# A 100-byte tile taken out of the constants of a one-core transformer block

## The chip, the cores and the metric

The kernel runs on one core of a Trainium2 chip. The metric is device microseconds of that core, from the first to the last work of one execution, and lower is better. Five kinds of worker appear in the profile: TensorE (PE for the matmuls, PEld for the loading of their weights), VectorE (DVE), ScalarE (ACT), GpSimd (POOL), and SyncE (SP), which issues nearly all transfers.

## The reference

One decoder layer on a sequence of 1024 tokens with 1024 features, in float32. What is computed, with the norms and reshapes left out:

```python
xn = rmsnorm(h, norm_mix_g)
proj = xn @ w_in                                  # 1024 x 2568: q, k, v, u, vg, forget gates
att = forgetting_attention(q, k, v, log_sigmoid(proj[..., G_END:] + b_forget))   # 8 heads of 64, causal
sg = chunked_spatial_gating(u, vg, v_gain, w_s, b_s)    # gelu(u) * (tril(w_s) @ rmsnorm(gelu(vg)) + b_s)
h = h + concatenate([att, sg]) @ w_out
a, g = split(causal_depthwise_conv3(rmsnorm(h) @ w_up) + conv_b)     # w_up: 1024 x 5632
h = h + (silu(g) * a) @ w_down                    # w_down: 2816 x 1024
out = rmsnorm(h)
```

## The kernel before

The kernel keeps float32 accuracy on TensorE by splitting every operand into a high part, rounded to the type float32r, and a low part, which is the operand less its high part. `split_w` does this for weights: a copy on ACT at line 392 and a subtraction on DVE at line 398. Each product then takes three matmuls: high by high, high by low, low by high. The large products are also cut into 2 x 2 blocks with seven block products in place of eight (Strassen's scheme, with the operands named A11 to S4 on the side of the weights and B11 to T4 on the side of the activations). So the matmuls come in runs of twelve (four blocks of 128 rows by three parts), nearly all with 128 rows, 128 columns of stationary weights and 512 columns of moving data.

The stages, in order of time:

- Projections (lines 495 and 637), to about 200 us. In `tmul`, line 495, the stationary operand is a block of x and the moving one is a block of weights. In `product`, line 637, it is the other way round. The split weights go through a ring of six buffers, `RTAG = ("wy", "wy", "whl", "whl", "whl", "whl")`.
- Attention (lines 1009 to 1058), gating, and the output projection, whose matmuls are worked in between as filling (line 1125, tile `fl`), to about 470 us.
- Up projection, 22 steps of seven products (`up_b` and `up_a`, line 1457, with convolution and SiLU on ACT and DVE). Weights A11 and A12 are in `wha`, the five others in `whb`; activations are in `xB11`, `xB21`, `xT2`, `xT3`, `xT1`, `xT4`, `xB22`. The order in a step is S2, S3, the A11 of the next step, S1, A22, the A12 of the next step, S4.
- Down projection (`dprod`, line 1652): seven products of 11 x 12 matmuls each, with `wha` stationary and `whb` moving.

The order of instructions up to the output projection is made by a planner (class `Pace`, method `settle`). It lists all instructions of this part, gives each a modelled duration, and simulates the engines; the order that it finds is then fixed for each engine. The later part runs in the order in which it is written.

On-chip memory is handed out by pools. The pools `cst` (constants), `sml`, `early`, `upl`, `xtp`, `pst` and `dn` lie on the left and grow upward; `raws`, `late` and `upr` lie on the right and grow downward from the top. In the allocation list of the program, addresses are bytes within each of the 128 partitions:

- Below 1152 lie a scratch area of 1024 bytes and four small constants.
- The constants take 2144 bytes, each tile rounded up to a multiple of 32: `cp` 768, `eps`, `one` and `lim` 32 each, `ident` 512, `maskb` 256, `pad` 128 (100 bytes rounded up), `ng1`, `rstd1` and `ss1` 32 each, `gms` 256, `ss2` 32.
- The small pool takes twelve tiles of 32 bytes. So `early`, and later `upl`, begin at 1152 + 2144 + 384 = 3680, which is 7 x 512 + 96.
- On the right, `raws` begins at 212960 = 415 x 512 + 480.

The tiles of `early`, `upl`, `late`, `raws` and `upr` that matmuls read all have sizes that are multiples of 512 bytes, and a slice of 128 float32 columns is 512 bytes. So every such operand on the left begins at the remainder 96 modulo 512, and every one on the right at 480 (the forget gates' weights at line 720, in steps of 256 bytes, are the exception). Which tile is where:

| left (96) | right (480) |
|---|---|
| `wy`, `gg`, `V`, `H`, `x1`, `x2`, `t2`, `t3`, `t01` | `whl`, `pt`, `A`, `G`, `raw` |
| `xB11`, `xB21`, `xT2`, `xT3`, `wha`, `sg` | `xT1`, `xT4`, `xB22`, `whb` |

`ident`, the identity matrix for transposes, lies among the constants at 2016, ahead of `pad`, with remainder 480. `pad` at line 370 is written once, by a memset on DVE at line 371, and read by nothing.

Of the kernel before, what the change touches and what calls it, by code (L numbers as in the profile page):

```python
# [8 lines left out]
F32 = mybir.dt.float32  # L9
# [5 lines left out]
P = 128  # L15
# [275 lines left out]
def block_kernel(ctx: ExitStack, tc: tile.TileContext, xT, xtok, wuv, wv, wqk, wf, cpk, bfv,  # L291
                 ggain, g2r, gfr, wsp, woa, wos, wup, wdn, out):
    nc = tc.nc
    act, dve, pool, pe, sp = nc.scalar, nc.vector, nc.gpsimd, nc.tensor, nc.sync
    pace = Pace(tc)

    cst = pace.pool(ctx.enter_context(tc.tile_pool(name="cst", bufs=1)))
# [69 lines left out]
    pool.affine_select(out=maskb, in_=maskb, pattern=[[-1, P]], compare_op=ALU.is_ge,  # L367
                       fill=BIG, base=0, channel_multiplier=1)

    pad = cst.tile([P, 25], F32, name="pad")  # L370
    dve.memset(pad, 0.0)
    ng1 = cst.tile([P, 8], F32, name="ng1")
    dve.tensor_scalar(out=ng1, in0=g1, scalar1=-1.0, scalar2=None, op0=ALU.mult)
    rstd1 = cst.tile([P, 8], F32, name="rstd1")
# [1420 lines left out]
```

## Time and profile before

| | |
|---|---|
| median of the runs | 1088.05 us (1086.39 to 1088.16, 3 runs) |
| profiled execution, its own time | 1090.22 us |
| profiled execution, span | 1088.5 us |
| granted TensorE clock, mean | 0.993 |

The span goes from the first to the last instruction of the profiled execution; its own time also holds what lies around it. In rows of the profile that name tiles, the tile written stands left of the arrow and those read right of it; a matmul's row names the moving operand first and the stationary one second (`b<-wy,V`: `wy` moves, `V` is stationary), and only one name where both come from tiles of the same name.

### The profile page before, as it was taken

What the parts mean: (1) busy time and instruction counts of PE and PEld (TensorE: products, weight loads), DVE (VectorE), ACT (ScalarE), POOL (GpSimd) and SP (SyncE); (2) the same over time, 40 slices, a digit from 0 to 9 for tenths busy, and PEclk for the clock granted to TensorE, in tenths of its full rate; (3) what the DMA queues carried; (4) which work ended last, traced back from release to release, by engine and by line L of the source; (5) the groups of instructions that cost most, each with busy time, mean ns of one, the idle gap of its engine ahead of it and who ended that gap; (6) DMA issues with size and microseconds to landing.
All of it is one profiled execution on the core that took longest, in us unless ns stands there. A gap on an engine that the chain in (4) does not pass through costs nothing.

```text
span 1088.5 us, 14285 instructions
## 1 busy us (share of the span) xinstructions
PE 1067.7 (98%) x4885; PEld 867.8 (80%) x4885; DVE 906.9 (83%) x1391; ACT 574.4 (53%) x1006; POOL 239.5 (22%) x211
## 2 busy tenths in 40 slices
PE   9999999999999999998999999999999999999997
PEld 6888778788888877876888888888888888888885
DVE  6986599898888868998888998988989766897774
ACT  6657444477777746653444445344444544453653
POOL 0002124233362250063233233333332000000000
PEclk9999999999999999998999999999999999999999
DMA  9242236886674354222313323331322998333432
GB/s 338 87 141 96 89 112 170 257 265 184 191 226 146 120 200 164 76 80 98 136 59 117 115 94 100 107 118 67 119 104 76 304 329 276 107 97 93 141 117 94
DMA packets 64712, 158.16 MB, mean 145 GB/s; under 512 B 7672, under 2 KB 7936, under 8 KB 64640
## 3 DMA queue, kind: packets, MB, share of 16 engines
q1 hardware_dynamic: 64352, 156.70, 43.7%
q8 instruction: 38, 0.62, 0.2%
q10 hardware_dynamic: 288, 0.56, 0.1%
q14 instruction: 34, 0.28, 0.1%
HBM read 114.95 MB, written 42.27 MB: 144 GB/s over the span
## 4 chain that ended last, share of the span: by engine, by line
PE 83%; issue 7%; DVE 4%; DMA 3%; POOL 2%; ACT 1%; SPq 0%; POOLq 0%; DVEq 0%; ACTq 0%
PE s L1457 20%; PE b L1457 14%; PE s L1652 11%; PE b L1652 8%; PE s L495 6%; PE b L495 5%; PE fl L1125 4%; PE po L1049 3%; PE tr L1030 3%; PE b L637 2%; PE s L637 2%; PE lg L1010 2%; PE lg L1009 2%; DMA qd<-G 1%; PE s L720 1%
## 5 line engine op out<-in xcount | busy, mean ns | idle before, releaser
L1457 PE MATMUL s<-xT,whb 128*128 128x512 f32 x804 | 191.6, 391 | 0.0
L1457 PEld LDWEIGHTS s<-xT,whb 128*128 128x128 f32 x804 | 150.9, 188 | 33.6 <-DVE u L1519 0.4
L1457 PE MATMUL b<-xB,wha 128*128 128x512 f32 x528 | 128.4, 392 | 2.1 <-DVE wha L398 2.1
L1652 PE MATMUL s<-whb,wha 128*128 128x512 f32 x528 | 123.2, 395 | 0.0
L1457 PEld LDWEIGHTS b<-xB,wha 128*128 128x128 f32 x528 | 99.1, 188 | 24.2 <-DVE wha L398 2.5
L1652 PEld LDWEIGHTS s<-whb,wha 128*128 128x128 f32 x528 | 99.5, 188 | 23.2
L392 ACT CAST wha<-sg 128x512 fp32r<-128x512 f32 x77 | 47.7, 620 | 101.6 <-PE b L1652 48.2
L392 ACT CAST whb<-sg 128x512 fp32r<-128x512 f32 x82 | 50.4, 615 | 81.1 <-PE s L1457 72.3
L1652 PE MATMUL b<-whb,wha 128*128 128x512 f32 x396 | 92.5, 395 | 0.0
L398 DVE TENSOR_TENSOR wha<-sg,wha 128x512 fp32r<-128x512 f32 x77 | 52.8, 688 | 45.2 <-ACT wha L392 44.7
L1652 PEld LDWEIGHTS b<-whb,wha 128*128 128x128 f32 x396 | 74.6, 188 | 17.4
L1125 PE MATMUL fl<-whl,H 128*128 128x512 f32 x192 | 71.5, 416 | 0.0
L1457 PE MATMUL s<-xB,whb 128*128 128x512 f32 x264 | 66.0, 400 | 4.4 <-DVE h L1529 4.4
L398 DVE TENSOR_TENSOR whb<-sg,whb 128x512 fp32r<-128x512 f32 x82 | 62.6, 764 | 9.0 <-ACT whb L392 8.7
L1457 PEld LDWEIGHTS s<-xB,whb 128*128 128x128 f32 x264 | 51.2, 194 | 15.8 <-DVE h L1529 4.9
L1457 PE MATMUL b<-xT,whb 128*128 128x512 f32 x252 | 62.4, 395 | 0.0
L1344 POOL TENSOR_TENSOR sg<-raw 128x512 f32<-128x512 f32 x20 | 28.3, 1414 | 147.3 <-DVE whb L398 84.3
L1049 PE MATMUL po<-pt,V 128*128 128x512 f32 (+1 forms) x192 | 58.7, 364 | 1.3 <-DVE pt L1041 1.3
L1041 DVE TENSOR_TENSOR pt<-tr,pt 128x512 fp32r<-128x512 f32 (+2 forms) x96 | 51.8, 550 | 8.7 <-ACT pt L1036 8.1
L1036 ACT CAST pt<-tr 128x512 fp32r<-128x512 f32 (+3 forms) x96 | 45.3, 474 | 25.8 <-PE tr L1030 23.2
L1457 PEld LDWEIGHTS b<-xT,whb 128*128 128x128 f32 x252 | 47.2, 188 | 11.3 <-DVE whb L398 0.3
L1345 POOL TENSOR_TENSOR sg<-sg,raw 128x512 f32<-128x512 f32 x20 | 41.3, 2063 | 62.7 <-issue 62.6
(383 smaller groups left out, 2344.5 us busy)
## 6 DMA issues: line engine op xcount, KB each, us to landing
raw<-wup SPq DMA_DIRECT2D x44, 512.0 KB, 3.6
sg<-hx SPq DMA_DIRECT2D x77, 256.0 KB, 2.6
hx<-hs SPq DMA_DIRECT2D x44, 256.0 KB, 2.2
hx<-ca SPq DMA_DIRECT2D x33, 256.0 KB, 2.0
xT<-wdn SPq DMA_DIRECT2D x28, 256.0 KB, 5.4
raw<-wqk SPq DMA_DIRECT2D x8, 512.0 KB, 3.9
qd<-G SPq DMA_DIRECT2D x16, 256.0 KB, 9.8
kd<-G SPq DMA_DIRECT2D x16, 256.0 KB, 3.2
```

Source lines behind the costliest of these rows:

```text
L392: act.copy(h, src)
L398: return eng.tensor_tensor(out=l, in0=src, in1=f32(h), op=ALU.subtract)
L495: pe.matmul(banks[m], xs(n, xi, k)[:, ms], w[:, wi, :], start=(first and k == 0 and c == 0), stop=(k == 3 and c == 2), skip_group_check=True)
L637: pe.matmul(ps, w[:, wi, ks], xs(n, xi, k), start=(first and c == 0), stop=(c == 11), skip_group_check=True)
L1030: pe.transpose(ps[:, (q - 4 * hf) * P:(q - 4 * hf + 1) * P], self.t[q][:, k * P:(k + 1) * P], ident)
L1036: act.copy(pt[:, 0, o:512], ps[:, o:512])
L1041: dve.tensor_tensor(out=pt[:, 1, o:512], in0=ps[:, o:512], in1=f32(pt[:, 0, o:512]), op=ALU.subtract)
L1049: pe.matmul(self.po[hf][:, o:512], lhs, pt[:, s, o:512], start=(k == 0 and s == 0), stop=(k == 4 * hf + 3 and s == 1), skip_group_check=True)
L1125: pe.matmul(self.bank, sgT[k][:, xi, ts_], self.w[hf, k][:, wi, :], start=(k == 0 and i == 0), stop=(k == 3 and i == 2))
L1345: pool.tensor_tensor(out=s[1], in0=s[0], in1=a11, op=ALU.add)
L1457: pe.matmul(ps, w[:, wi, ks], xb[:, xi, k, :], start=(first and n == 0), stop=(n == 11), skip_group_check=True)
L1652: pe.matmul(banks[bk + m], xh[:, xi, ms], wh[:, wi, :], start=(first and p_ == 0 and n == 0), stop=(p_ == NP - 1 and n == 2), skip_group_c ...
```

## The change

The tile `pad` and its memset are taken out. Nothing else is edited. The constants become 128 bytes shorter, so `ng1`, `rstd1`, `ss1`, `gms`, `ss2`, the small pool and all pools on the left move down by 128 bytes: `early` and `upl` begin at 3552 = 6 x 512 + 480. What lies ahead of `pad` and everything on the right stay where they are. DVE has one instruction less.

```diff
     pool.affine_select(out=maskb, in_=maskb, pattern=[[-1, P]], compare_op=ALU.is_ge,
                        fill=BIG, base=0, channel_multiplier=1)
 
-    pad = cst.tile([P, 25], F32, name="pad")
-    dve.memset(pad, 0.0)
     ng1 = cst.tile([P, 8], F32, name="ng1")
     dve.tensor_scalar(out=ng1, in0=g1, scalar1=-1.0, scalar2=None, op0=ALU.mult)
```

## Prediction, written before the changed kernel ran

> **What bounds the kernel now.** I read the page first (busy shares), then the chain of waits, then the waits of TensorE, and then went to single products in the timeline.
>
> ```profile
> span 1088.5 us, 14285 instructions
> PE 1067.7 (98%) x4885; PEld 867.8 (80%) x4885; DVE 906.9 (83%) x1391; ACT 574.4 (53%) x1006; POOL 239.5 (22%) x211
> ```
>
> TensorE is busy for 98% of the span, so the time hangs on the rate at which it starts matmuls. The chain of waits, cut to one step of the up projection, gives that rate. Its columns are start, time and what; a piece is a run of matmuls of one line into one kind of bank.
>
> ```profile
> 660.70 2.80 PE s L1457 x12
> 663.49 2.77 PE b L1457 x12
> 666.26 5.45 PE s L1457 x24
> 671.71 2.73 PE b L1457 x12
> 674.44 2.72 PE s L1457 x12
> 677.16 2.79 PE b L1457 x12
> 679.96 2.80 PE s L1457 x12
> ```
>
> All seven products do the same work, yet they do not take the same time. In order these are S3, A11 of the next step, S1 with A22, A12, S4, S2, and the next S3. S2 and S3 multiply `whb` (right pool) by `xT2` or `xT3` (left pool): 2.79 and 2.80 us, or 233 ns a matmul. S1, A22 and S4 have both operands on the right: 5.45/24 = 227 and 2.72/12 = 226.7 ns. A11 and A12 have both on the left: 2.77 just after the slow S3, and 2.73 further on. The down projection has a left operand (`wha`) and a right one (`whb`) everywhere, and is slow everywhere:
>
> ```profile
> 867.03 30.67 PE b L1652 x132
> ...
> 989.73 30.68 PE b L1652 x132
> 1020.41 55.09 PE s L1652 x237
> ```
>
> 30.67/132 = 232.3 ns and 55.09/237 = 232.4 ns. The cleanest comparison is in the projections, where the timeline shows two runs of 22 matmuls of one line, with the two halves of one stationary operand, a few us apart:
>
> ```profile
> 84.41 5.30 PE L495 MATMUL b<-whl,V 128*128 128x512 f32 x22
> ...
> 90.00 5.17 PE L495 MATMUL b<-wy,V 128*128 128x512 f32 x22
> ```
>
> `V` is on the left. With moving `whl` (right) 22 matmuls take 5.30 us, with `wy` (left) 5.17: 0.13/21 = 6 ns for each further matmul. In all these runs the weights of the next matmul are loaded while the present one streams (PEld is busy 868 us beside PE), so two reads of on-chip memory run side by side. The reading that fits every row: a matmul costs 226.7 ns when the two reads stand at one remainder modulo 512, and some 232 to 233 when they stand 128 or 384 bytes apart (480 against 96). Distance by itself does nothing: `wy` at 124512 and this `V` at 13920 are 108 KiB apart and fast, `xT1` and `whb` 48 KiB and more apart and fast. The up and down projections never wait; the longest waits of TensorE lie before 496 us:
>
> ```profile
> PE s L1457 <- DVE h L1529: 4.4, 1, 4.4
> PE b L1457 <- DVE wha L398: 2.1, 1, 2.1
> PE s L495 <- DVE G L889: 1.9, 1, 1.9
> ```
>
> **The change, part by part.** First the memset.
>
> ```profile
> 1.17 0.08 DVE L371 MEMSET pad<- 128x25 f32 x1
> ...
> 2.36 0.06 DVE L362 MEMSET lim<- 128x1 f32 x1 [1.11 <-ACT lim L357]
> ```
>
> It takes 0.08 us, and DVE then idles 1.11 us until ACT is done with `lim`. It saves nothing at the end: the first real matmul starts at 6.42 us, behind the transfers of x and weights. At most it is 0.08 us. The planner would see the same gap, so I take its order as unchanged.
>
> Then the move of the left pools by 128 bytes, from remainder 96 to 480. It adds and removes no wait, transfer or step. Each matmul pair that stood at 96 against 480 now stands at 480 against 480. What such a left-right pair costs the trace does not show. Its near ends are 226.7 ns (same pool, same remainder) and 232.3 to 233.3 (as now). I take 226.7, because both kinds of same-pool pair, left with left and right with right, reach 226 to 227 at all distances. Above the dear end nothing is shown; a rival below prices that. By stage:
>
> - *Down projection.* Five pieces of 132 and one of 237 are 897 matmuls on the chain. (232.4 - 226.7) x 897 = 5.1 us, all on the path. The tail after 1075.5 us stays.
> - *Up projection.* A step of seven products is 679.96 - 660.70 = 19.26 us; seven times 2.72 are 19.04, so 0.22 a step. From the wide window below, 1609 matmuls are 1609/84 = 19.2 steps: 4.2 us.
> - *Projections to 141 us.* In the window from 17.96 to 104.49 us the chain holds 374 matmuls, 86.53/374 = 231.4 ns, so 4.7 x 374 = 1.75 us; 0.2 for the 49 before it, and 4.7 x 150 = 0.7 for the wide ones after it (166 less 16 narrow). Together 2.6 us.
> - *141 to 207 us.* Here the chain goes through DVE's gating work and through transfers, so I count nothing; the upper end is 270 x 4.7 = 1.3 us.
> - *Attention, 207 to 450 us.* Mixed wide matmuls are the filling and the wide part of `po`: 288 x 5.7 = 1.6 us. PE's turn there alternates with waits for DVE and ACT; I take half, 0.8 (ends 0 and 1.6).
> - *450 to 496 us.* PE is busy 39.46 of 46 us and waits for DVE; nothing.
>
> ```profile
> 17.96:104.49 86.53, 86.53 (x375) 1.00 0.41 144
> 104.49:141.00 36.51, 35.99 (x166) 1.00 0.25 73
> 141.00:207.00 66.00, 62.98 (x270) 1.00 0.62 180
> 450.00:496.00 46.00, 39.46 (x170) 0.98 0.33 109
> 496.00:867.00 371.00, 371.00 (x1609) 0.99 0.33 112
> 203.00:215.00 12.00, 10.11 (x38) 0.86 0.59 190
> 490.00:503.00 13.00, 8.55 (x27) 0.74 0.43 147
> ```
>
> (These are windows of PE: window, length, busy with count, granted clock, DMA share, GB/s.)
>
> ```profile
> L1125 PE MATMUL fl<-whl,H 128*128 128x512 f32 x192 | 71.5, 416 | 0.0
> L1049 PE MATMUL po<-pt,V 128*128 128x512 f32 x96 | 34.8, 417 | 0.0
> ```
>
> The other engines must follow a TensorE that runs 1 to 2% faster. What hides this is that they wait for it now:
>
> ```profile
> L392 ACT CAST wha<-sg 128x512 fp32r<-128x512 f32 x77 | 47.7, 620 | 101.6 <-PE b L1652 48.2 <-PE s L1652 42.4 <-issue 9.2
> L392 ACT CAST whb<-sg 128x512 fp32r<-128x512 f32 x82 | 50.4, 615 | 81.1 <-PE s L1457 72.3 <-POOL sg L1345 3.7 <-PE b L1457 3.3
> L398 DVE TENSOR_TENSOR whb<-xT,whb 128x512 fp32r<-128x512 f32 x49 | 32.9, 684 | 0.0
> L398 DVE TENSOR_TENSOR wha<-sg,wha 128x512 fp32r<-128x512 f32 x77 | 52.8, 688 | 45.2 <-ACT wha L392 44.7
> ```
>
> In the down projection ACT sits idle 90.6 us (48.2 + 42.4) until a matmul frees a `wha` buffer, so transfers and casts are ahead of need; were that cover gone, the 5.1 us would shrink towards nothing. The same rows show that ACT and DVE do not care about remainders: a cast from left to left is 620 ns, from left to right 615; DVE's subtraction into the left pool 688, into the right one 684, at most 0.8 us in all for the 159 of both kinds, beside other work.
>
> The sum: 5.1 + 4.2 + 2.6 + 0.8 = 12.7 us. Durations come from the profiled execution (own time 1090.22, span 1088.5), which stands 2.2 us over the median, so it should go to about 1077.5. From the median of 1088.05: 1075.3 us.
>
> At one place a rule of the Trainium skill speaks against all this. "TensorE: Matmul & The Clock Gate", in the section "Step-by-step: what each phase is for", says that the streaming operand and the weight load have independent read ports, and "Loading the next tile's weights doesn't steal SBUF read bandwidth from the running matmul." By that rule remainders could not matter and the sum would be zero, 1088.05 us. The rows of 5.30 against 5.17 us disagree with it as far as they go.
>
> **The rivals.**
>
> *The slow pairs are slow because they cross pools, not because of remainders.* Before, every pair of unequal remainders was also a pair of left and right, so the trace cannot part the two. For it: that. Against it: fast pairs span 108 KiB within the left pool, so no short-range bank of memory explains "side". If so, nothing changes: 1088 us. This is also what the quoted rule forecasts, and the case in which the change does nothing that counts.
>
> *The stages before 496 us swallow their share.* They hold waits on DVE and transfers (rows above), and a gain ahead of such a wait may only lengthen it. Then only 5.1 + 4.2 = 9.3 us come through: 1078.7 us.
>
> *Left-right pairs at one remainder are dearer still* (slower). If crossing pools is what collides, the same remainder may make it collide in every line. At least 897 + 2/7 x 1609 = 1357 matmuls from 496 us on are such pairs, all without waits. Each ns more costs 1.36 us, so it shows as slower from 1.6 ns on. If it adds as much again as the present 5.7 ns: +7.7 us there, some 1096 us. Against it: every pair at one remainder that the trace shows is fast.
>
> *The planner finds another order* without the memset. It covers the part to about 470 us, where PE now waits for several us; a worse order could double that. It would have to add over 12.7 us to turn the sign, and the gap around the memset speaks against any change.
>
> **How the numbers follow.** Forecast 0.74; swallowed 0.11; crossing pools 0.09; dearer pairs 0.05; another order 0.01. About 0.2%, 2.2 us, is what a measurement of this kernel can tell from no change. Faster is the first two with some of the last, 0.85; same 0.09; slower 0.06. The range of the likeliest: the ends of the terms give gains from 11.9 to 14.8 us. Besides, the clock was granted at 0.86 in the 12 us around 207 and at 0.74 in the 13 us around 495, after PE stood idle: 1.7 and 3.4 us lost. When the idle stretches shift, one may vanish or another come, so I allow 3.3 us downward: 1070.0. Upward, 1078.7 of the second case and as much again: 1082.0. The two cases at 1088 and above stay outside.
>
> **What would show it right or wrong.** In the profile after: S2 and S3 at 2.72 us per twelve, a step near 19.04 to 19.08 us, 132 matmuls of the down projection in 29.9 us, runs of 22 with `whl` and `wy` alike; casts and subtractions unchanged; PE's waits before 496 us about as long as now. If the step stays at 19.26 and the 132 at 30.67, sides matter and not remainders. If these fall and the total does not, the first part has grown waits.

## The result, and the profile after

The changed kernel takes 1075.49 us (median of 4 runs, 1074.76 to 1076.24) against 1087.46 for the kernel before over the same comparison (4 runs, 1086.39 to 1088.16). The ratio is 0.9891, 95% interval 0.9874 to 0.9908: faster by 12.0 us. The prediction was 1075.3.

The profiled execution of the changed kernel has a span of 1074.3 us and a time of its own of 1075.99. Line numbers are two lower than before. Its page:

```profile
span 1074.3 us, 14284 instructions
PE 1053.2 (98%) x4885; PEld 865.8 (81%) x4885; DVE 905.7 (84%) x1390; ACT 574.8 (54%) x1006; POOL 238.9 (22%) x211
```

One instruction is gone, the memset. The busy time of PE fell by 14.5 us, that of DVE and ACT stayed: the same work, but TensorE gets through it sooner. One step of the up projection in the chain of waits (start, time, what):

```profile
678.33 5.44 PE s L1455 x24
683.77 2.72 PE b L1455 x12
686.49 2.72 PE s L1455 x12
689.21 2.72 PE b L1455 x12
691.93 2.72 PE s L1455 x12
694.65 2.72 PE b L1455 x12
697.37 5.44 PE s L1455 x24
```

Every product now takes 2.72 us per twelve, also S2 and S3, which took 2.79 and 2.80. A step is 697.37 - 678.33 = 19.04 us, before 19.26. The down projection in the same view:

```profile
857.85 29.92 PE b L1650 x132
...
1007.45 53.80 PE s L1650 x237
```

29.92/132 = 226.7 ns in place of 232.3. And the two runs of 22 in the projections, in the timeline:

```profile
83.09 5.15 PE L493 MATMUL b<-whl,V 128*128 128x512 f32 x22
...
88.53 5.15 PE L493 MATMUL b<-wy,V 128*128 128x512 f32 x22
```

`whl` against `V`, across the pools, now costs the same as `wy` against `V`, within one pool. PE's waits before 496 us are the same ones, each within 0.4 us of its length before, and one more of 0.2 us; the longest, 4.4 us before:

```profile
PE s L1455 <- DVE h L1527: 4.6, 1, 4.6
```

### The profile page after: what moved, and what is told of

Read it like the earlier page. It is cut to its first block, busy times and chain, and to the rows that moved or that the text cites. A ratio compares the mean times of both kernels' runs of the same rounds, so it can differ in the third digit from the quotient of the medians.

```text
span 1074.3 us, 14284 instructions
## 1 busy us (share of the span) xinstructions
PE 1053.2 (98%) x4885; PEld 865.8 (81%) x4885; DVE 905.7 (84%) x1390; ACT 574.8 (54%) x1006; POOL 238.9 (22%) x211
## 4 chain that ended last, share of the span: by engine, by line
PE 82%; issue 7%; DVE 5%; DMA 3%; POOL 2%; ACT 1%; SPq 0%; POOLq 0%; DVEq 0%; ACTq 0%
PE s L1455 20%; PE b L1455 14%; PE s L1650 11%; PE b L1650 8%; PE s L493 6%; PE b L493 5%; PE fl L1123 4%; PE po L1047 3%; PE tr L1028 3%; PE b L635 2%; PE s L635 2%; PE lg L1008 2%; PE lg L1007 2%; DMA qd<-G 1%; DMA x<-kd 1%
## 5 line engine op out<-in xcount | busy, mean ns | idle before, releaser
L1650 PE MATMUL s<-whb,wha 128*128 128x512 f32 x528 | 120.2, 389 | 0.0
L1650 PE MATMUL b<-whb,wha 128*128 128x512 f32 x396 | 90.2, 389 | 0.0
```

The lines of the kernel that those rows point to most:

```text
L1650: pe.matmul(banks[bk + m], xh[:, xi, ms], wh[:, wi, :], start=(first and p_ == 0 and n == 0), stop=(p_ == NP - 1 and n == 2), skip_group_c ...
```

## The experiments

The theory to be tested is that a float32r matmul is slow when its moving operand and the weights loaded at the same time stand at unequal remainders, on whichever side of memory they are. The rivals are the left pools' absolute place, the crossing of pools, other engines' traffic, the memset, and a modulus other than 512.

**The right side moved instead of the left** (edit of the kernel before; `pad` and its memset stay; the release of the pool at the end is left out here)

```diff
+    rpad = tc.alloc_tile_pool(name="rpad", bufs=1, side="right")
+    rpad.tile([P, 96], F32, name="rpad")
     raws = pace.pool(tc.alloc_tile_pool(name="raws", bufs=1, side="right"))
```

> The kernel before with its pad and memset kept; instead 384 bytes are taken at the top of the right side, so that the right pools go down to remainder 96, where the left ones are. Remainder theory: the same gain as the change, ratio 0.989 (0.987 to 0.991), S2 and S3 at 2.72 us per twelve, 132 matmuls of the down projection in 29.92 us. Rival, it is the left pools' absolute place at 480 (or the shorter constants) that counts: ratio 1.000, 2.79 and 30.67 us.

Measured: 1075.19 us against 1086.38, ratio 0.9898 (0.9883 to 0.9913). Its chain of waits:

```profile
673.98 2.72 PE b L1459 x12
...
856.22 29.92 PE b L1654 x132
```

The same gain with everything at 96 and with the constants as long as before. So it is the relation of the two sides that counts, not the place of either.

**A pair within one pool made unequal** (edit of the changed kernel)

```diff
     for n in ("B11", "B21", "T2", "T3"):
         xb_tile(upl, n)
+    upl.tile([P, 32], F32, name="shift")
```

> The changed kernel with 128 bytes put between the xT3 and wha tiles, so that wha and sg begin at remainder 96 and all else at 480. Now A11 and A12, whose two operands both lie in the left pool, stand 384 bytes apart, and so does the down projection; S1 to S4 and A22 stay equal. Remainder theory: A11 and A12 at 2.78 to 2.80 us per twelve instead of 2.72, the down projection back at 30.67 us per 132; together 0.15 x 20 + 5.1 = some 8 us over the changed kernel, ratio to before 0.996 (0.994 to 0.998). Rival, only pairs across the pools pay: A11 and A12 stay at 2.72, only the down projection (if anything) is slow, 5.1 us, ratio 0.9935 or below.

Measured: 1083.14 us, ratio 0.9971 (0.9959 to 0.9984) against 1086.38 for the kernel before: 3.2 us are left of the 12.0 that the change gave. Its chain of waits, A12 and S4, then S3 and A11, and a piece of the down projection:

```profile
664.20 2.80 PE b L1456 x12
667.00 2.75 PE s L1456 x12
...
672.47 2.73 PE s L1456 x12
675.19 2.80 PE b L1456 x12
...
859.59 30.67 PE b L1651 x132
```

A12 and A11, with both operands in the left pool, now take the longest, 2.80, and S2 and S3, across the pools, are fast at 2.72 and 2.73. The rival that only crossing pairs pay falls. S4, which follows A12, is not quite at 2.72 (2.75). It may be that the rate takes some matmuls to settle after a slow product, as in the A11 at 2.77 of the kernel before; no run tests this. With these neighbours a step is at 19.26 us again, 0.22 over the changed kernel, where 0.15 was expected.

**The memset alone** (edit of the kernel before)

```diff
     pad = cst.tile([P, 25], F32, name="pad")
-    dve.memset(pad, 0.0)
```

> The kernel before without the memset of pad, the tile itself kept: one half of the change alone. Theory: the memset lay in idle time of DVE, so nothing, ratio 0.999 to 1.001, 30.67 us per 132. Rival, the memset's place in DVE's order mattered for the start or for the planner: part of the 12 us comes.

Measured: 1086.68 us against 1086.88, ratio 0.9999 (0.9990 to 1.0009); a piece of 132 takes 30.67 us. The memset is worth nothing that this comparison can see; the gain is the 128 bytes.

**Matmuls alone, offset by offset** (a kernel of its own, one execution: one line of matmuls, `st` and `mv` at one remainder, `off` in bytes)

```python
for r in range(48):
    k = r % 6
    pe.matmul(ps, st[:, k * P:(k + 1) * P], mv[:, off // 4:off // 4 + 512], ...)
```

> This kernel computes nothing of the block: it only multiplies, 21 groups of 48 float32r matmuls (128 x 128 stationary, 512 moving, six stationary blocks in turn), with the moving operand 0, 16, 32, ... 512 and again 0 bytes past the stationary one modulo 512, and no other engine or transfer at work beside it. Remainder theory: 226.7 ns a matmul (10.88 us a group) at 0 and 512, 229 to 236 ns (11.0 to 11.3 us) at 128 and 384; between them the trace has shown nothing, but the period should be 512. Rival, the reads disturb each other only while other engines write too: all groups alike within 0.5 ns. Rival, the port rule (independent reads): all groups alike as well.

In the timeline each group of 48 is one row; from its start to that of the next row, divided by 48, is the time of a matmul. Groups g and h are the offsets 128 and 160, k and l are 256 and 288, s, t and u are 496, 512 and 0.

```profile
75.25 11.36 PE L39 MATMUL offg<-mv,st 128*128 128x512 f32 x48
86.45 11.40 PE L39 MATMUL offh<-mv,st 128*128 128x512 f32 x48
...
120.07 11.05 PE L39 MATMUL offk<-mv,st 128*128 128x512 f32 x48
130.96 11.37 PE L39 MATMUL offl<-mv,st 128*128 128x512 f32 x48
...
209.19 11.05 PE L39 MATMUL offs<-mv,st 128*128 128x512 f32 x48
220.08 11.08 PE L39 MATMUL offt<-mv,st 128*128 128x512 f32 x48
231.00 11.04 PE L39 MATMUL offu<-mv,st 128*128 128x512 f32 x48
```

At 128: (86.45 - 75.25)/48 = 233.3 ns; at 256: (130.96 - 120.07)/48 = 226.9; at 512: 227.5. (At 64, by the same view, 229.2.) No other engine works here but ACT, which copies each finished group out in 0.59 us, so the cost does not need the traffic of others. That TensorE's two reads disturb each other is inferred from the cost going by the distance between the two operands; no run leaves the loading of weights out. And 256 is as cheap as 0: the modulus in the words of the change, 512, is too large by a factor of two. At 384, the distance in the down projection before, the sweep has 233.3 where the kernel before had 232.3; this 1 ns is not explained.

**256 and 32 bytes in the whole kernel** (edit of the changed kernel, 64 or 8 columns)

```diff
+    cst.tile([P, 64], F32, name="pad")
     ng1 = cst.tile([P, 8], F32, name="ng1")
```

> The changed kernel with an unwritten tile of 256 bytes at the place of the old pad: the left pools begin at 224, the right ones at 480 modulo 512. Theory of a period of 256: same gain as the change, ratio 0.989 to 0.990, 2.72 us per twelve everywhere and 29.92 us per 132. Rival, the period is 512 as in the words of the change: the gain is gone, ratio 1.000, S2 and S3 at 2.79, 30.67 us.

> The changed kernel with an unwritten tile of 32 bytes there: left pools at 0, right ones at 480. By the sweep's 32 and 480 (233.5 and 233.1 ns) the pairs cost as much as before, or up to 1 ns more: S2 and S3 2.79 to 2.81 us, 132 matmuls of the down projection 30.7 to 30.9 us, ratio 0.999 to 1.002. Rival, nearness of the remainders is enough: some of the gain stays, ratio 0.995 or below.

Measured: with 256 bytes 1075.17 us against 1086.88, ratio 0.9892 (0.9874 to 0.9911); with 32 bytes 1089.73, ratio 1.0032 (1.0020 to 1.0043). The chain of waits with 256, then with 32:

```profile
672.64 2.72 PE s L1456 x12
...
857.60 29.92 PE b L1651 x132
```

```profile
669.69 2.75 PE b L1456 x12
672.44 2.75 PE s L1456 x12
...
865.74 30.79 PE b L1651 x132
```

256 bytes apart is as good as equal. 32 bytes apart is a little worse than the kernel before, more than expected in the total (at most 1.002): 30.79/132 = 233.3 ns, within what the sweep has at 32 and 480 (233.5 and 233.1). S2 and S3 take 2.80 each, as expected, but the products with equal pairs are slower too: A12 and S4, the two upper rows, take 2.75, before 2.73 and 2.72. A11, S1, A22 and A12 lie between S3, the last product with unequal pairs, and S4, so slow settling does not explain this by itself; why is open.

**Finer steps**

> Matmuls alone again, 26 groups of 48, the moving operand 0, 4, 8, 12, 16, 20, 24, 28, 60, 64, 68, 72, 80, 128, 224, 228, 232, 236, 240, 244, 248, 252, 256, 320, 496 and 0 bytes past the stationary one. The first sweep had 0, 256, 496 and 512 at 227 ns, 64 and 320 at 229, all else at 231 to 234. Theory of a period of 256 bytes: 240 is as 496 (227 ns), 64 as 320 (229), and there is a cheap stretch from 240 to 256, so 244, 248 and 252 at 227 too; 4 to 12 between 227 and 231.5. Rival, a period of 512 with accidental equals at 256: 240 at 233 where 496 is at 227. An offset below 226 ns would open a way to a faster kernel; none is expected.

Rows s, t and u are 240, 244 and 248; x, y and z are 320, 496 and 0.

```profile
209.57 11.51 PE L39 MATMUL offs<-mv,st 128*128 128x512 f32 x48
220.93 11.68 PE L39 MATMUL offt<-mv,st 128*128 128x512 f32 x48
232.44 11.21 PE L39 MATMUL offu<-mv,st 128*128 128x512 f32 x48
...
265.27 11.17 PE L39 MATMUL offx<-mv,st 128*128 128x512 f32 x48
276.28 11.50 PE L39 MATMUL offy<-mv,st 128*128 128x512 f32 x48
287.61 11.07 PE L39 MATMUL offz<-mv,st 128*128 128x512 f32 x48
```

In part a miss. 320 is at 229.4 as 64 was, which agrees with a period of 256. But 240 is at 236.7 and not 227, 244 at 239.8, 248 at 230.0, and 496 at 236.0, where the first sweep had 226.9 for the same offset. So of the cheap stretch below 256 only 252 is left (227.1 in the same view), and at 496 the offset alone does not fix the rate. Above 0, too, 4 and 8 are at 236.7 and 233.1, where at most 231.5 was expected. 28 is at 226.7 and 60 at 226.9. No offset is below 226.6, so none makes a faster kernel.

**Both operands moved alike, and bf16**

> Again matmuls alone. First six groups in which both operands are moved together by 0, 32, 64, 128, 256 and 384 bytes: the remainder theory has only the difference count, so all six at 226.7 ns (10.88 us for 48). Rival, the absolute start counts: some of them slower, 229 ns or more. Then 15 groups of bf16 with the moving operand 0 to 512 bytes past the stationary one: a bf16 stationary block is 256 bytes for each partition, so if the period is that of the stationary block's row, 0 and 256 are alike; if it is 512, they differ. No size is forecast for bf16.

Rows alikeb and alikec are 32 and 64 bytes for both operands; halfg and halfh are bf16 at 128 and 160.

```profile
19.53 11.08 PE L46 MATMUL alikeb<-mv,st 128*128 128x512 f32 x48
30.45 11.07 PE L46 MATMUL alikec<-mv,st 128*128 128x512 f32 x48
...
136.23 10.52 PE L46 MATMUL halfg<-bm,bs 128*128 128x512 bf16 x47
146.59 10.52 PE L46 MATMUL halfh<-bm,bs 128*128 128x512 bf16 x47
```

Moved alike by 32 bytes, (30.45 - 19.53)/48 = 227.5 ns, and 226.9 to 227.7 for the others: only the difference counts. (The first group, at 0, starts after TensorE stood idle and took 280.0 ns; it tells nothing.) In bf16 the offsets give 10.36/48 = 215.8 ns throughout (216.0 in the first group): float32r shows the effect, bf16 does not.

**What went before, and narrower blocks**

> Matmuls alone. First part: the offset 496 is tried again after 0, 480, 320, 128, 0 and 28, since it gave 226.8 ns after 480 in one sweep and 236.2 ns after 320 in another. Theory, two steady states and the matmuls before choose: 226.7 after 480 again, 236 after 320 again, after 0 most likely 226.7. Rival, the two runs differ by chance: no tie to what went before. Second part, a stationary block of 128 columns with 384, 256 and 128 moving columns, and 512 moving columns with a block of 64 and of 32 columns, each at offset 0 and 128. Theory, the loading of weights and the stream disturb each other for as long as the loading lasts: the extra cost at 128 (6.7 ns with 512 and 128 columns) stays at 384 and 256 moving columns, and falls to about a half and a quarter with 64 and 32 stationary columns. Rival, the extra goes by the length of the stream: three quarters and a half of it at 384 and 256, the same at 64 and 32 stationary columns. At 128 moving columns the loading alone should set the rate (108 ns), offset or not.

Row pastd is the offset 496 after 480; widec and wided 384 moving columns at 0 and 128, widee and widef 256 columns; widei and widej 64 stationary columns at 0 and 128.

```profile
41.94 11.36 PE L44 MATMUL pastd<-mv,st 128*128 128x512 f32 x48
53.14 11.15 PE L44 MATMUL paste<-mv,st 128*128 128x512 f32 x48
...
164.27 8.49 PE L44 MATMUL widec<-mv,st 128*128 128x384 f32 x48
172.59 8.61 PE L44 MATMUL wided<-mv,st 128*128 128x384 f32 x48
181.04 5.92 PE L44 MATMUL widee<-mv,st 128*128 128x256 f32 x48
186.80 5.86 PE L44 MATMUL widef<-mv,st 128*128 128x256 f32 x48
192.50 5.47 PE L44 MATMUL wideg<-mv,st 128*128 128x128 f32 x48
...
203.17 11.20 PE L44 MATMUL widei<-mv,st 128*64 128x512 f32 x48
214.21 11.26 PE L44 MATMUL widej<-mv,st 128*64 128x512 f32 x48
225.31 11.27 PE L44 MATMUL widek<-mv,st 128*32 128x512 f32 x48
```

Neither theory holds. 496 after 480 is at (53.14 - 41.94)/48 = 233.3, not 226.9 as in the first sweep; after 320 it is 236.0 again. After 0, tried twice, it is at 233.3 and not at the 226.7 expected, and after 28 at 236.5. So this offset has at least three rates, and the one group before does not choose among them by itself; what does stays open. The extra at 128 is 6.6 ns with 512 moving columns, 2.7 with 384 (173.3 and 176.0) and -1.3 with 256 (120.0 and 118.8): it shrinks faster than the stream. With 64 stationary columns there is no cheap case at these two offsets, 230.0 at 0 and 231.3 at 128; with 32 columns, 231.5 at 0. With 128 moving columns the rate is 110.6 at 0 and 111.7 at 128, near the 108 expected.

## Why the prediction was right

*The mechanism.* The step on which all hung, that a left-right pair at one remainder costs what a same-pool pair costs, is shown: 226.7 ns in the products of both large projections, the gain again with the right side moved, the loss in a same-pool pair moved apart. Why unequal remainders cost time inside TensorE is not shown.

The rule quoted from the Trainium skill ("TensorE: Matmul & The Clock Gate", "Step-by-step: what each phase is for") does not hold for float32r here: by it the place of the operands could not matter, and the sweep has 233.3 ns at 128 bytes against 226.9 at 256 by their distance alone. For bf16, at 215.8 ns for all offsets, the runs show nothing against it.

*The terms*, by the two profiled executions, in us:

| stretch | forecast | measured | from |
|---|---|---|---|
| down projection | 5.1 | 5.1 | 867.03 to 1075.50, now 857.85 to 1061.25 |
| up projection | 4.2 | 4.1 | 371.31, now 366.16, less 1.04 of clock |
| to 141 us | 2.6 | 2.3 | 141.01, now 138.73 |
| 141 to 207 us | 0 | 0.9 | 66.11, now 65.18 |
| 207 to 496 us | 0.8 | 0.8 | 288.60, now 287.78 |
| sum | 12.7 | 13.2 | and 1.04 of clock: 14.2, the spans' difference |

The stretches before 496 us begin and end with these rows of the chain of waits, of the kernel before and then of the changed one:

```profile
141.01 0.70 DVE G L889
...
207.12 4.61 PE s L495 x12
...
495.72 5.38 PE s L1457 x12
```

```profile
138.73 0.70 DVE G L887
...
203.91 4.61 PE s L493 x12
...
491.69 4.34 PE s L1455 x12
```

One profile of each kernel cannot size the last two of these stretches. The profiles of the experiments serve as repeats: up to the up projection the kernel without the memset and the one with 32 bytes have unequal pairs, as before, and those with the right side moved, with 256 bytes and with the same-pool pair moved apart have equal ones, as the changed kernel has. The same rows of their chains give, in us:

| stretch | unequal pairs | equal pairs |
|---|---|---|
| to 141 us | 141.01, 141.28, 141.59 | 138.73, 138.55, 138.93, 138.06 |
| 141 to 207 us | 66.11, 65.12, 65.84 | 65.18, 65.91, 65.39, 65.42 |
| 207 to 496 us | 288.60, 285.36, 285.86 | 287.78, 285.36, 286.87, 285.48 |

To 141 us the means differ by 2.7, and the forecast of 2.6 was right. From 141 to 207 us the two groups overlap, so the 0.9 above is no gain that was overlooked, and counting nothing there was sound. From 207 to 496 us they overlap as well and spread over 3.2 us: whether the attention stage passed on half of its share, all of it or nothing is not shown, and that 0.8 came out in one pair of profiles is luck.

*The total.* The gain was 12.0 us by the medians (10.0 to 13.7 by the interval), the forecast 12.7. The time of 1075.49 came within 0.2 us of the forecast partly by luck: the kernel before had 1087.46 in this comparison, and the sum was taken from 1088.05.

*The clock.* The last rows above differ by 5.38 - 4.34 = 1.04 us for the same twelve matmuls: they run after PE's idle stretch, at a granted clock of 0.52 before and 0.67 after. They are an S4 (`xB22` by `whb`, both on the right), an equal pair in every kernel, so their own remainders do not make the difference. Over the seven profiles they take 4.34 to 5.38 us at a clock of 0.67 to 0.52. The three kernels that have unequal pairs up to here have the three longest times (5.03 to 5.38, the others 4.34 to 4.61); whether that is chance is open. At 207 us the time varies whatever the pairs: the twelve matmuls that take 4.61 us above, at a clock of 0.63, take 3.05 in the kernel without the memset, at 1.00.

The profiled execution of the kernel before stands 2.8 us over the median of this comparison and that of the changed kernel 0.5 over, so the spans differ by 14.2 us where the medians differ by 12.0. Putting the sum on the median, not on the profile, was right, and the allowance of 3.3 us for the clock was of the right kind.

*The rivals.* The order of instructions on every engine is the same in both profiles but for the memset, and the memset alone gave 0.9999. "Crossing pools" and "dearer pairs" fell with the change itself and with the pair made unequal within one pool. "Swallowed before 496 us" would have been 1078.7, above every run of the changed kernel (1076.24 at most); in the profiles the up projection starts at 493.6 us in the mean with unequal pairs and at 490.4 with equal ones, though the nearest two are 491.76 and 491.69.

*The covers.* ACT still waits for PE in the down projection, and its casts moved by 3 ns, which shows nowhere:

```profile
L390 ACT CAST wha<-sg 128x512 fp32r<-128x512 f32 x77 | 48.0, 623 | 97.1 <-PE b L1650 46.0
```

*What was wrong in the reasoning.* "Modulo 512" was taken over from the tiles at hand, which only showed differences of 0, 128 and 384. The sweep and the kernel with 256 bytes put the period at 256. "Distance by itself does nothing" is borne out only for whole multiples of it, such as the 108 KiB of the example; what is left over modulo 256 decides. The forecast did not hang on either.

## What to carry to other kernels

When TensorE is the bound and runs of the same matmul differ by a few ns, sort them by where their two operands lie before looking for waits: here one row of 22 against another of 22 gave the size of the gain beforehand. With float32r, 128 stationary columns and 512 moving ones, give all operand tiles one remainder modulo 256 bytes, the only difference that was cheap in whole kernels too; a small constant tile that shifts one side of memory can cost a percent without a wait showing anywhere. Take the unit price from equal runs side by side and multiply only over stages in which the engine never waits.

## What the runs showed of the hardware that was not expected

- The cost needs nothing but TensorE's matmuls with their weight loads, and it goes by the distance between the two operands: 226.7 to 227.5 ns at 0, 28, 60, 252, 256 and 512 bytes (48 matmuls in a row, without the first group of each kernel), 229 at 64 and 320, 233 at 32, 96, 128, 192 and their like 256 further on, up to 240.0 at 20.
- The period is 256 bytes, not the 512 of a stationary row: 32, 64, 96, 128, 160, 192 and 224 bytes each ran within 0.2 ns of the offset 256 further on, in one sweep.
- The offset does not always fix the rate: 496 ran at 226.9, 233.3 and 236.0 ns in different sequences. Why is open.
- The cheap case was seen with the full block only: with 64 stationary columns offset 0 took 230.0 ns, with 256 moving columns the offset 128 was the cheaper by 1.3 ns.
- bf16 ran at 215.8 ns at every offset, so even the best float32r matmul, at 226.7, is 10.9 ns slower, with the same 512 columns.
